# Program order on every engine for a seven-product encoder kernel, with its stages rewritten one run of twelve products apart

## The chip, the cores and the metric

The kernel runs on one core of one Trainium2 chip. The core has TensorE (PE in the profile; its weight loads are PEld), VectorE (DVE), ScalarE (ACT), GpSimd (POOL) and SyncE (SP, which here issues all DMAs). The engines work side by side and wait for each other through semaphores. The metric is the device time of one execution in microseconds, and lower is better.

## The reference

The reference is one layer of an encoder trunk on 2048 frames of 1024 features in float32. All branches read one normalised input through one projection, and their outputs go through one output projection:

```python
h = _rmsnorm(x, norm_w[layer])
proj = h @ w_in[layer]
...
y_a = _conv_mixer(a_h, a_b, a_c, a_z, conv_a_w[layer])
y_b = _gla_mixer(g_q, g_k, g_v, g_lr, g_z, gla_gate_w[layer], gla_gate_b[layer], gla_norm_w[layer])
y_c = _pool_mixer(p_u, p_z, pool_w[layer], pool_scale[layer])
y_d = _ssd_mixer(s_xbc, s_dt, s_z, ssd_conv_w[layer], ssd_conv_b[layer], ssd_dt_bias[layer],
                 ssd_a_log[layer], ssd_d[layer], ssd_norm_w[layer])
mix = jnp.concatenate([y_a, y_b, y_c, y_d], axis=-1)
x = x + mix @ w_out[layer]
...
return _rmsnorm(x, final_norm_w)
```

The conv branch is a causal convolution with gates. The gla and ssd branches carry a state from chunk to chunk of 64 frames (outer products within a chunk, a decayed sum over chunks, a product with the state). The pool branch takes running means over 2, 4, 8 and 16 frames. Each branch is gated by a SiLU of its own part of the projection.

## The kernel before

**Precision.** Every large product is made of three: both factors are split into a high and a low part (`split`: ACT casts the high part, DVE subtracts it to get the low part), and PE multiplies low by high, high by high and high by low. A product over 512 inputs is thus twelve matmuls of 128x512 (`mm12`, line 224), called a run here.

**Seven products.** Two projected blocks of 128 outputs, over two halves of 512 frames and two halves of the 1024 inputs, form a 2x2 block product. `pair7` makes it with seven runs instead of eight. `prep7` loads the four weight blocks of a pair, forms their sums on POOL (lines 200 to 210) and splits the seven left factors; the seven right factors (b11, t2, b21, t1, t3, t4, b22) stand in the dictionary `H`. `first7` makes the first run of the next pair ahead of time, into an accumulator a. Each pair begins by copying the negated a into a second accumulator b on ACT (line 240); b is then accumulated by three more runs, with a partial result read out between them (`cp2`, `cp3`, `ev21`), a by one more (`ev11`), and a third accumulator e by two (read by two subtractions, lines 252 and 262). A pair has 84 matmuls.

**Stages.** The frames go in two segments of 1024. In each segment a first phase multiplies by ordinary threes for the values, the gates and the time steps (`outer4`, `block_tok`), while `rows_gen` builds the right factors in `H`. Then follow the ten pairs of `PAIRS`: qk, B, xs, C (with a convolution and a SiLU each for the last three, `ssd_conv`), a_h, a_c, a_b, a_z (`a_pair`), p_u (`pu_pair`), p_z (`pz_pair`). From a_h on `chunk_loop` runs beside them: `update` makes a tile's state updates on PE, `advance` moves the states on by DVE and POOL, `outputs` multiplies by them on PE. `gate_outputs` norms and gates the results, and `to_mix` transposes them on PE and writes them to DRAM. After the second segment come eight more pairs, two rows of 128 frames each, for the output projection; `square` and `emit` make the last norm and write the rows. Their right factors come from `wout_gen`.

**Order.** The code is written as a series of runs with a call of `tick()` after each. A tick takes one step of each generator that is set (`chunks`, `prep_`, `side`) and then starts what `later(n, fn)` had put off by n ticks. So the program order mixes the work of several stages. It isn't the order of execution: a scheduler of the tile framework goes through the program with its own model of durations and puts each engine's instructions into an order, a ready instruction ahead of one that its model has still waiting. Only at few places is an order written by hand, with `issue_after` (`gate_decay`, `fin_B`). Whatever the order, an engine then runs its list one after the other.

The functions that the change touches, before it:

Of the kernel before, what the change touches and what calls it, by code (L numbers as in the profile page):

```python
# [9 lines left out]
F32 = mybir.dt.float32  # L10
# [7 lines left out]
P = 128  # L18
# [13 lines left out]
NW = 20  # L32
NG = 10
# [22 lines left out]
def tile_hybrid_trunk(ctx: ExitStack, tc: tile.TileContext, xtok, xT, wkv, wch, wpu, wz, wo, pw_, nw, par, gw, fnw, out):  # L56
    nc = tc.nc
    vec, act, pe, sp, pool = nc.vector, nc.scalar, nc.tensor, nc.sync, nc.gpsimd
# [134 lines left out]
    def prep7(load, w7):  # L193
# [4 lines left out]
        w7.append(split_w(a11))  # L198
# [4 lines left out]
        yield 1  # L203
        w7.append(split_w(s2))
        pool.tensor_add(a21, a21, a11)  # L205
        yield 1
        w7.append(split_w(a12))
        yield 1
        w7.append(split_w(a21))
        pool.tensor_add(a12, a12, s2)  # L210
        yield 1
        w7.append(split_w(s1))
        yield 1
        w7.append(split_w(a22))
        yield 1
        w7.append(split_w(a12))
        yield 1
# [10 lines left out]

    def first7(w7, H):

        a = acc()
        mm12(a, w7[0], H['b11'], True)
        ahead[0] = a
        tick()

    def pair7(w7, H, ev11, ev21, d12, d22, cp2, cp3, done, after=None):
# [12 lines left out]
        tick()  # L249
        e = acc()  # L250
        mm12(e, w7[4], H['t1'], True)
# [3 lines left out]
        mm12(b, w7[5], H['t4'], False)  # L255
# [3 lines left out]
        if after is not None:  # L259
            after()  # L260
        mm12(e, w7[6], H['b22'], False)
# [68 lines left out]
    def fold_pu(j):  # L330

        wt_ = [wt("wr", F32) for _ in range(2)]
        for h in range(2):
            sp.dma_start(wt_[h], wpu[j][:, h * 512:(h + 1) * 512])
# [3 lines left out]
        def fold(h):  # L338
            tp = tr()
            for i in range(4):  # L340
                pe.matmul(tp[:, i * P:(i + 1) * P], lhsT=wt_[h][:, i * P:(i + 1) * P], rhs=mix, start=True, stop=True)
# [4 lines left out]
        later(4, lambda: fold(1))  # L346
# [79 lines left out]
    def transposed(t, fn, lag=4):  # L426
# [8 lines left out]
    def chunk_loop(kv, kt, q, aG, aD, bt, xs, wt_, cc, after):  # L435
# [3 lines left out]
        def update(tt):  # L439
            wx = psm.tile([P, 4, CH], F32, tag="wx", name=nm("wx"), bufs=2)  # L440
# [3 lines left out]
            wx = wx.rearrange("p h c -> p (h c)")  # L444
# [39 lines left out]
        st = None  # L484
        for tt in range(TT):
            if tt:
                outputs(tt - 1, st)
            ups = update(tt)
            st = [advance(tt, i, ups[i]) for i in range(2)]
            for _ in range(TPT):  # L490
                yield 1
        outputs(TT - 1, st)

    def gate_outputs(s, f, kv, xs, rt):
# [4 lines left out]
        szs = []  # L499
        for i, tt in enumerate(ts4):  # L500
# [3 lines left out]
        ro = rsqrt(so.rearrange("p a b -> p (a b)"), 1.0 / CH, 16)  # L504
# [602 lines left out]
```

## Time and profile before

| | |
|---|---|
| Time, median of 3 runs | 871.24 us (869.7 to 872.1) |
| Time of the profiled execution | 871.0 us, of which 869.0 us is the span of the profile |
| Busy, of the span | PE 777.5 us, DVE 650.8 us, ACT 407.6 us, POOL 249.8 us |
| Mean granted TensorE clock | 0.955 |
| DMA | 94.08 MB, 108 GB/s |

The span reaches from the first to the last instruction. Busy time is the time in which an engine had an instruction under way; a matmul's end is modelled, and matmuls overlap. The first phase ends at 93.7 us, the first pair at 128.0, the other nine at 354.2; the second segment's first phase ends at 435.4, its ten pairs at 667.8. The output projection takes the rest.

### The profile page before, as it was taken

Reading aid. Unit: us, or ns where it says so; the run is one execution under the profiler, and the core shown is the slowest. Engines: PE = TensorE matmul, PEld = TensorE weight load, DVE = VectorE, ACT = ScalarE, POOL = GpSimd, SP = SyncE. Lnnn points to the kernel's source line nnn. Section 1 sums busy time; section 2 is a strip of 40 time slices with the busy share of each in tenths; the row PEclk is TensorE's granted clock in tenths of the full one; section 3 lists DMA queues with packets and bytes.
Section 4 is the critical chain, followed back from the end, with each engine's and each line's share of the span. In section 5 each row is a group of like instructions: output and inputs, shape, how many; then the busy total and the mean of one; then the engine's idle time right before and its main releaser. Section 6 shows DMA issues by size and latency. Waiting matters only on the chain. (4 is left out here: it accounts for less than half of the span.)

```text
span 869.0 us, 11534 instructions
## 1 busy us (share of the span) xinstructions
PE 777.5 (89%) x3944; PEld 628.3 (72%) x3944; DVE 650.8 (75%) x1252; ACT 407.6 (47%) x804; POOL 249.8 (29%) x206
## 2 busy tenths in 40 slices
PE   6999599999995998799999999989988479999985
PEld 5988378878774786687878877767867357777774
DVE  4779965776699689873835776797779988777775
ACT  6646526663562554353536664334554523333331
POOL 0003622335433120220322245543126522222200
PEclk9999799999998999979999999999989699999998
DMA  8611211121551543322041111112733624444411
GB/s 287 231 66 61 97 49 49 48 77 57 175 184 49 178 163 110 100 75 83 25 142 54 49 49 50 41 58 89 257 115 98 193 90 168 143 148 152 149 48 73
DMA packets 57578, 94.08 MB, mean 108 GB/s; under 512 B 5840, under 2 KB 20656, under 8 KB 57008
## 3 DMA queue, kind: packets, MB, share of 16 engines
q1 hardware_dynamic: 57520, 93.35, 32.4%
q8 instruction: 31, 0.51, 0.3%
q14 instruction: 27, 0.22, 0.1%
HBM read 71.31 MB, written 22.02 MB: 107 GB/s over the span
## 5 line engine op out<-in xcount | busy, mean ns | idle before, releaser
L224 PE MATMUL acc<-hl,wh 128*128 128x512 f32 x784 | 320.6, 409 | 52.8 <-DVE hl L151 22.7
L224 PE MATMUL acc<-hh,wl 128*128 128x512 f32 x784 | 312.4, 399 | 0.0
L224 PE MATMUL acc<-hh,wh 128*128 128x512 f32 x784 | 312.3, 398 | 0.0
L224 PEld LDWEIGHTS acc<-hl,wh 128*128 128x128 f32 x784 | 151.3, 193 | 95.7 <-DVE hl L151 16.9
L224 PEld LDWEIGHTS acc<-hh,wl 128*128 128x128 f32 x784 | 151.0, 193 | 33.0
L224 PEld LDWEIGHTS acc<-hh,wh 128*128 128x128 f32 x784 | 151.8, 194 | 29.4
L151 DVE TENSOR_TENSOR wl<-wr,wh 128x512 fp32r<-128x512 f32 (+1 forms) x172 | 119.9, 701 | 51.3 <-ACT wh L150 28.1
L150 ACT CAST wh<-wr 128x512 fp32r<-128x512 f32 (+1 forms) x172 | 101.7, 601 | 64.8 <-DVE wl L151 28.6
L200 POOL TENSOR_TENSOR ws<-wr,wr 128x512 f32<-128x512 f32 x28 | 42.5, 1520 | 272.9 <-PE acc L224 121.8
L151 DVE TENSOR_TENSOR wl<-ws,wh 128x512 fp32r<-128x512 f32 x56 | 42.8, 764 | 53.3 <-ACT wh L150 46.2
L150 ACT CAST wh<-ws 128x512 fp32r<-128x512 f32 x56 | 34.6, 618 | 92.6 <-POOL wr L205 55.3
L151 DVE TENSOR_TENSOR hl<-xq,hh 128x1024 fp32r<-128x1024 f32 (+1 forms) x52 | 72.6, 1426 | 2.2 <-ACT hh L150 2.1
L210 POOL TENSOR_TENSOR wr<-wr,ws 128x512 f32<-128x512 f32 x28 | 42.4, 1513 | 96.8 <-issue 77.2
L565 DVE SCALAR_TENSOR_TENSOR t<-xin,prm,t 128x512 f32<-128x512 f32 x72 | 58.3, 842 | 8.0 <-ACT t L563 8.0
L150 ACT CAST hh<-xq 128x1024 fp32r<-128x1024 f32 (+1 forms) x52 | 50.9, 1014 | 25.5 <-DVE xq L783 16.2
L302 PE MATMUL acc<-wl,hh 128*128 128x276 f32 (+1 forms) x160 | 55.5, 352 | 7.3 <-DVE wl L151 7.2
L966 ACT ACTIVATE xk<-r 128x512 f32<-128x512 f32 x32 | 20.2, 632 | 77.7 <-DVE r L1001 34.1
L302 PE MATMUL acc<-wh,hh 128*128 128x276 f32 (+1 forms) x160 | 50.0, 351 | 7.2 <-ACT wh L150 6.6
L302 PE MATMUL acc<-wh,hl 128*128 128x276 f32 (+1 forms) x160 | 54.4, 346 | 0.0
L783 POOL TENSOR_TENSOR xq<-xq,xq 128x1024 f32<-128x1024 f32 x10 | 28.9, 2896 | 62.7 <-DVE xq L783 48.5
L205 POOL TENSOR_TENSOR wr<-wr,wr 128x512 f32<-128x512 f32 x28 | 42.8, 1530 | 0.0
L302 PEld LDWEIGHTS acc<-wl,hh 128*128 128x128 f32 x160 | 32.5, 203 | 11.6 <-DVE wl L151 9.1
(219 smaller groups left out, 1104.8 us busy)
## 6 DMA issues: line engine op xcount, KB each, us to landing
wr<-in_wch SPq DMA_DIRECT2D x72, 256.0 KB, 3.4
xk<-in_xtok SPq DMA_DIRECT2D x64, 256.0 KB, 3.7
wr<-yd SPq DMA_DIRECT2D x32, 256.0 KB, 3.1
out<-r SPq DMA_DIRECT2D x32, 256.0 KB, 2.0
xq<-in_xT SPq DMA_DIRECT2D x14, 512.0 KB, 6.4
wr<-in_wz SPq DMA_DIRECT2D x16, 256.0 KB, 2.7
szd<-z SPq DMA_DIRECT2D x16, 256.0 KB, 2.4
sz<-szd SPq DMA_DIRECT2D x16, 256.0 KB, 3.1
```

The lines of the kernel that those rows point to most:

```text
L150: act.copy(hi, raw)
L151: vec.tensor_sub(lo, raw, hi.bitcast(F32))
L200: pool.tensor_add(s1, a21, a22)
L205: pool.tensor_add(a21, a21, a11)
L210: pool.tensor_add(a12, a12, s2)
L224: pe.matmul(o[:, cs], lhsT=a[:, ks], rhs=b[:, k, cs], start=start and k == 0 and i == 0, stop=k == KH - 1 and i == 2, skip_group_check=True)
L302: pe.matmul(o[tt][:, :n], lhsT=a[:, k % KH, sl], rhs=wts[k][b], start=k == 0 and i == 0, stop=k == KD - 1 and i == 2)
L565: vec.scalar_tensor_tensor(t, x[:, k:k + 512], pcol('scw', 4 * i + k), t, ALU.mult, ALU.add)
L783: eng.tensor_tensor(o[:, k:k + 2, :], x[:, k:k + 2, :], y[:, k:k + 2, :], op)
L966: act.activation(x[:, cs], r, AF.Square, accum_out=sq[:, i:i + 1])
```

## The change

**The order.** Each engine is wrapped in a class `Ordered`. While `strict[0]` is set, every instruction, DMA issues on SP and matmuls on PE among them, is tied behind the one that the program wrote before it on the same engine. It is set in each segment before its first pair, taken back after the first segment's last pair (so the second segment's first phase is ordered by the scheduler as before), and stays set from the second segment's pairs to the end. The `issue_after` in `fin_B` goes.

**The pair.** The seven runs of a pair, numbered here by the order in the new `pair7`, are: 1, s2 by t2 into b; 2, a12 by b21 into a; 3, s1 by t1 into e; 4, s3 by t3 into b; 5, the next pair's a11 by b11 (`first7`); 6, a22 by t4 into b; 7, s4 by b22 into e. A tick follows each, called tick 1 to 7. Before, run 4 stood ahead of run 3 and run 5 stood between 6 and 7. `prep7` issues its loads before the pair's first tick, does three of its four POOL sums in one step and makes one split per tick, and what is left is drained at the end of the pair, no longer before run 5.

**The rest.** `side` takes two steps per tick. Convolutions, SiLUs, transposes, the steps of `gate_outputs`, `emit` and `to_mix` get other distances in ticks. The chunk loop starts during C, takes two ticks per tile instead of three, and has `update` and `outputs` in different ticks; the tile `wx` has one buffer instead of two. `fold_pu` and `row_scale` for the second segment move from the pairs a_h and a_c into the first segment's first phase. The second segment's rows, or the output weights, are loaded and split from the end of a_z on. The weights of the second segment's first phase are fetched three ahead. The output pairs load their rows of x one pair ahead (`Rows`). The pool of 128x512 weight tiles goes from 20 to 18 buffers, the general one from 10 to 12. The arithmetic is the same.

```diff
-NW = 20
-NG = 10
+NW = 18
+NG = 12
...
+    strict = [False]
+    class Ordered:
...
+                if self.last is None:
+                    r = f(*args, **kw)
+                else:
+                    with tc.issue_after(self.last):
+                        r = f(*args, **kw)
+                self.last = r.ins
...
-        for g in (chunks, prep_, side):
+        for g in (chunks, prep_, side, side):
...
         a = ahead[0]
         b = acc()
         act.activation(b, a, AF.Copy, scale=-1.0)
-        mm12(b, w7[1], H['t2'], False)
+        mm12(b, w7['s2'], H['t2'], False)
         cp2(d12, b)
         tick()
-        mm12(a, w7[2], H['b21'], False)
+        mm12(a, w7['a12'], H['b21'], False)
         ev11(a)
         tick()
-        mm12(b, w7[3], H['t3'], False)
+        e = acc()
+        mm12(e, w7['s1'], H['t1'], True)
+        tick()
+        mm12(b, w7['s3'], H['t3'], False)
         cp3(d22, b)
-        tick()
-        e = acc()
-        mm12(e, w7[4], H['t1'], True)
         vec.tensor_sub(d22, d22, e)
         done(0)
         tick()
-        mm12(b, w7[5], H['t4'], False)
+        if after is not None:
+            after()
+            tick()
+        mm12(b, w7['a22'], H['t4'], False)
         ev21(b)
         done(1)
         tick()
-        if after is not None:
-            after()
-        mm12(e, w7[6], H['b22'], False)
+        mm12(e, w7['s4'], H['b22'], False)
         vec.tensor_sub(d12, e, d12)
         done(2)
         tick()
...
-    def transposed(t, fn, lag=4):
+    def transposed(t, fn, lag=2):
...
         st = None
+        wx = inputs(0)
+        yield 1
         for tt in range(TT):
             if tt:
                 outputs(tt - 1, st)
-            ups = update(tt)
+            yield 1
+            ups = update(tt, wx)
+            if tt + 1 < TT:
+                wx = inputs(tt + 1)
             st = [advance(tt, i, ups[i]) for i in range(2)]
-            for _ in range(TPT):
-                yield 1
+            yield 1
+        yield 1
         outputs(TT - 1, st)
...
-                later(1 + i, lambda tt=tt: to_mix(tt))
+                later(3 + i, lambda tt=tt: to_mix(tt))
...
+        later(3, scales_)
         for i, tt in enumerate(ts4):
-            later(1 + i, lambda i=i, tt=tt: gated(i, tt))
-        later(6, finish)
+            later(1 + i // 2, lambda i=i, tt=tt: squares(i, tt))
+            later(2 + i, lambda i=i, tt=tt: fetch(i, tt))
+            later(4 + i, lambda i=i, tt=tt: gated(i, tt))
+            later(5 + i, lambda i=i, tt=tt: sums(i, tt))
+        later(9, finish)
...
             for k in (2, 1, 0):
                 vec.scalar_tensor_tensor(t, x[:, k:k + 512], pcol('scw', 4 * i + k), t, ALU.mult, ALU.add)
-            fin(j, f, t)
+            later(1, lambda: fin(j, f, t))
...
             if j == 1:
-                conv(1, 1)
+                later(2, lambda: conv(1, 1))
             elif j == 2:
-                conv(0, 1)
+                later(2, lambda: conv(0, 1))
...
                 act.activation(t, u[:, 2:514], AF.Copy, scale=pcol('caw', 3 * j + 2))
-                for k in (1, 0):
-                    vec.scalar_tensor_tensor(t, u[:, k:k + 512], pcol('caw', 3 * j + k), t, ALU.mult, ALU.add)
+
+                def taps():
+                    for k in (1, 0):
+                        vec.scalar_tensor_tensor(t, u[:, k:k + 512], pcol('caw', 3 * j + k), t, ALU.mult, ALU.add)
+                later(1, taps)
...
                 elif j == 2:
-                    conv(0, 1)
+                    later(1, lambda: conv(0, 1))
...
-            with tc.issue_after(last_exp[0].ins):
-                act.activation(t, t, AF.Silu)
+            act.activation(t, t, AF.Silu)
...
+                    later(6, lambda: side.__setitem__(0, chain(next_wout(), pause(2), wout_gen(Hw))))
...
+        def done(self, j):
+            if j == 0:
+                square(self.r[1][1], self.x[1][1], self.sq[1], 0)
+            elif j == 1:
+                later(2, lambda: emit(self.tt + 1, self.rows[1], self.sq[1]))
+            else:
+                square(self.r[0][1], self.x[0][1], self.sq[0], 1)
+                if self.tt + 2 < NTT:
+                    later(3, lambda: emit(self.tt, self.rows[0], self.sq[0]))
+                else:
+                    emit(self.tt, self.rows[0], self.sq[0])
```

## Rows read from the trace of the kernel before

**Rows 1.** Busy time and clock by stretch; the columns stand in its first line.

```profile
core 0: us, PE busy (x) PEld busy (x) DVE busy (x) ACT busy (x) POOL busy (x), PEclk, DMA share, GB/s
...
93.70:128.00 34.30, 23.79 (x84) 18.27 (x85) 28.36 (x23) 14.51 (x22) 14.94 (x7) 0.80 0.27 89
128.00:354.20 226.20, 209.58 (x1171) 167.23 (x1171) 175.34 (x379) 123.61 (x252) 68.15 (x65) 0.97 0.33 107
354.20:435.40 81.20, 74.72 (x396) 65.15 (x395) 54.81 (x75) 34.49 (x64) 18.70 (x11) 0.94 0.24 71
435.40:667.80 232.40, 222.77 (x1202) 177.84 (x1201) 168.44 (x330) 113.51 (x224) 82.46 (x73) 0.98 0.28 94
667.80:711.20 43.40, 23.64 (x85) 17.96 (x84) 40.04 (x38) 19.62 (x28) 19.18 (x9) 0.84 0.38 117
711.20:840.90 129.70, 120.50 (x505) 96.10 (x504) 98.39 (x227) 43.91 (x98) 32.85 (x24) 0.97 0.40 140
```

**Rows 2.** PE's waits over the whole span: total, times, longest.

```profile
PE tr L529 <- DVE xs L521: 13.6, 3, 8.4
PE acc L224 <- DVE r L1010: 10.3, 6, 3.2
```

**Rows 3.** Timeline of PE from 271 us: start, length, instruction.

```profile
270.77 0.39 PE L224 MATMUL acc<-hh,wh 128*128 128x512 f32 x1
...
272.13 0.39 PE L224 MATMUL acc<-hh,wh 128*128 128x512 f32 x1
...
282.49 0.69 PE L529 MATMUL tr<-prm,xs 128*128 128x128 f32 x2 [8.35 <-DVE xs L521]
```

**Rows 4.** Groups on ACT by form: busy, mean ns, idle before.

```profile
L563 ACT ACTIVATE t<-xin,prm 128x512 f32<-128x512 f32 x24 | 18.9, 814 | 2.9 <-DVE xin L262 2.9
L240 ACT ACTIVATE acc<-acc 128x512 f32<-128x512 f32 x28 | 16.3, 582 | 9.8 <-PE acc L224 9.8
...
L611 ACT ACTIVATE ah<-u,prm 128x512 f32<-128x512 f32 x8 | 5.6, 717 | 3.2 <-DVE u L608 3.2
L899 ACT ACTIVATE t<-t 128x512 f32<-128x512 f32 x8 | 5.1, 633 | 2.9 <-DVE t L565 2.8
```

**Rows 5.** Timeline of DVE from 136 us.

```profile
147.49 4.11 DVE L565 SCALAR_TENSOR_TENSOR t<-xin,prm,t 128x512 f32<-128x512 f32 x6 [1.18 <-ACT t L563]
...
152.11 0.68 DVE L262 TENSOR_TENSOR xin<-acc,xin 128x512 f32<-128x512 f32 x1
```

**Rows 6.** Timeline of ACT from 710 us.

```profile
710.77 0.63 ACT L966 ACTIVATE xk<-r 128x512 f32<-128x512 f32 x1 [1.92 <-DVE r L1005]
711.31 0.18 ACT L966 ACTIVATION_READ_ACCUMULATOR xk<-r 128x1 f32 x1
711.40 0.58 ACT L240 ACTIVATE acc<-acc 128x512 f32<-128x512 f32 x1
711.92 0.60 ACT L150 CAST wh<-wr 128x512 fp32r<-128x512 f32 x1
```

**Rows 7.** Short stretches: a gap of PE and the time behind it.

```profile
583.00:586.50 3.50, 0.03 (x1) 0.00 (x0) 3.33 (x8) 1.01 (x4) 1.48 (x3) 0.99 0.00 0
586.50:589.90 3.40, 3.38 (x8) 2.70 (x9) 2.79 (x4) 2.58 (x5) 1.25 (x1) 0.51 0.02 5
```

**Rows 8.** Timeline of DVE from 655 us.

```profile
662.60 1.22 DVE L783 TENSOR_TENSOR xq<-xq,xq 128x1024 f32<-128x1024 f32 x1
...
668.29 2.31 DVE L783 TENSOR_TENSOR t<-xq,xq 128x1024 f32<-128x1024 f32 x1
...
684.84 14.54 DVE L151 TENSOR_TENSOR hl<-xq,hh 128x1024 fp32r<-128x1024 f32 x8
```

**Rows 9.** Timeline of DVE from 850 us, where the last row is written.

```profile
862.83 0.15 DVE L138 TENSOR_SCALAR na<-sq 128x1 int32<-128x1 int32 x1
...
864.56 1.41 DVE L976 SCALAR_TENSOR_TENSOR r<-r,ny,fw 128x512 f32<-128x512 f32 x2
```

**Rows 10.** Timeline of POOL from 655 us.

```profile
667.78 1.74 POOL L210 TENSOR_TENSOR wr<-wr,ws 128x512 f32<-128x512 f32 x1
```

More of the change, by code (lines that the diff above doesn't have):

```diff
@@ L345, in fold_pu @@
         later(2, lambda: fold(0))
-        later(4, lambda: fold(1))
+        later(3, lambda: fold(1))
     last_exp = [None]
@@ L498, in gate_outputs, with squares @@
         sy = psm.tile([P, 4], F32, tag="sy", name=nm("sy"))
-        szs = []
-        for i, tt in enumerate(ts4):
+        ro = []
+        szs = {}
+        def squares(i, tt):
             sq = gen("sq")[:, :256]
@@ L788, in chain, with pause @@
             yield from g
+    def pause(n):
+        for _ in range(n):
+            yield 1
     def half_gen(f):
@@ L879, in tile_hybrid_trunk @@
             spill_z(tt, o)
-        w7 = []
+        w7 = {}
         prep_[0] = prep7(load_pair(PAIRS[0]), w7)
+        if s + 1 < NSEG:
+            fold_pu(0)
+            later(3, lambda: fold_pu(1))
+            for f in range(2):
+                scales[2 * s + 2 + f] = psm.tile([P, 4], F32, tag="rt2", name=nm("rt2"))
+                later(2 + 3 * f, lambda f=f: row_scale(2 * s + 2 + f, scales[2 * s + 2 + f]))
         o = [acc() for _ in range(4)]
@@ L934, in tile_hybrid_trunk @@
                 prep_[0] = prep7(load_rows(0), w_next)
-            if name == 'a_h':
-                chunks[0] = chunk_loop(kv, kt, q, aG, aD, bt, xs, wt_, cc, after_chunks)
-                if s + 1 < NSEG:
-                    later(1, lambda: fold_pu(0))
-                    later(6, lambda: fold_pu(1))
-            if name == 'a_c' and s + 1 < NSEG:
-                for f in range(2):
-                    scales[2 * s + 2 + f] = psm.tile([P, 4], F32, tag="rt2", name=nm("rt2"))
-                    later(1 + 4 * f, lambda f=f: row_scale(2 * s + 2 + f, scales[2 * s + 2 + f]))
-            if name == 'p_u':
-                side[0] = next_rows(s + 1) if s + 1 < NSEG else next_wout()
-            if name == 'p_z':
-                drain(side)
-                side[0] = half_gen(0) if s + 1 < NSEG else wout_gen(Hw)
+            if w_next is not None and not (n + 1 == len(PAIRS) and s + 1 < NSEG):
+                next(prep_[0])
+            if name == 'C':
+                later(3, lambda: chunks.__setitem__(0, chunk_loop(kv, kt, q, aG, aD, bt, xs, wt_, cc, after_chunks)))
+            if name == 'a_z':
+                if s + 1 < NSEG:
+                    later(6, lambda: side.__setitem__(0, chain(next_rows(s + 1), pause(8), half_gen(0))))
+                else:
+                    later(6, lambda: side.__setitem__(0, chain(next_wout(), pause(2), wout_gen(Hw))))
             def after():
-                drain(prep_)
-                if w_next:
-                    first7(w_next, H if n + 1 < len(PAIRS) else Hw)
-            pair7(w7, H, *consumers(name), after=after)
+                first7(w_next, H if n + 1 < len(PAIRS) else Hw)
+            pair7(w7, H, *consumers(name), after=after if n + 1 < len(PAIRS) or s + 1 == NSEG else None)
+            drain(prep_)
             w7 = w_next
         drain(side)
+        strict[0] = s + 1 == NSEG
     NTT = SEQ // P
@@ L1022, in after @@
-        def after():
-            drain(prep_)
-            if w_next:
-                first7(w_next, H)
-        pair7(w7, H, ev11, ev21, r[0][1], r[1][1], cp2, cp3, done, after=after)
+            next(prep_[0])
+            later(3, lambda: nxt.append(Rows(tt + 2)))
+        rows.take()
+        pair7(w7, H, rows.ev11, rows.ev21, rows.r[0][1], rows.r[1][1], rows.cp2, rows.cp3, rows.done,
+              after=(lambda: first7(w_next, H)) if tt + 2 < NTT else None)
+        drain(prep_)
         w7 = w_next
+        rows = nxt[0] if nxt else None
@@ L1030, in _pack @@
+    while queue:
+        tick()
 def _pack(x, norm_w, w_in, conv_a_w, gla_gate_w, gla_gate_b, gla_norm_w, pool_w, pool_scale, ssd_conv_w, ssd_conv_b,
```

170 lines of the change are left out of this document (95 added, 75 removed).

## The prediction

> **What bounds the kernel now.** I read the busy time by stretch first, cut where the kernel's stages begin [rows 1]. PE is busy nearly throughout, so time is lost only where PE stands or runs at the lower clock. I count a stretch's loss as its length less PE's busy time, plus (1 - granted clock) times that busy time. It is 10.5 + 4.8 = 15.3 us in the first pair, 16.6 + 6.3 = 22.9 in the first segment's other nine, 6.5 + 4.5 = 11.0 in the second segment's first phase, 9.6 + 4.5 = 14.1 in its ten pairs, 19.8 + 3.8 = 23.6 in the first output pair, 9.2 + 3.6 = 12.8 in the next six: 99.7 us in all. The rest is matmuls that the change keeps.
>
> PE's waits say who is late [rows 2]: transposes that stood too early in PE's order for DVE, and the read of a partial result (cp2) on DVE. The timeline shows what one such place does [rows 3]: PE stood for 8.35 us at a transpose. From 270.77 to 272.13 us six matmuls start, one each 0.227 us, so a run takes 2.72 us.
>
> A gap also costs afterwards. PE stood for 3.5 us at clock 0.99, and the next 3.4 us ran at 0.51, the lower of the two levels (1.2 and 2.4 GHz) [rows 7]. That costs another 1.7 us.
>
> **What the change takes away.** The new stages put transposes two or more ticks behind what they read, and cp2 two runs ahead of the run that overwrites it. I count the losses of the three stretches of pairs as gone, 22.9 + 14.1 + 12.8 = 49.8 us (the rows leave 0 to 49.8). The weights of the second segment's first phase are split earlier: 7 of its 11.0 us. Two steps of `side` per tick bring the first pair's right factors forward, but DVE is busy for 28.4 of its 34.3 us [rows 1]: 7.3 of 15.3.
>
> The first output pair is a queue on DVE: eight low parts of right factors take 14.54 us in a row, 1.82 each [rows 8]. There are 14 of them and four sums for DVE. They move to nine ticks of p_u and p_z, two steps per tick, beside four window sums and the weight splits. Two steps at 1.22 to 1.82 are 2.4 to 3.6 us, a whole run for DVE before its other work. So most of the queue stays, now in p_u and p_z: I keep 14 of 23.6 us and take off 9.5. Gone in all: 49.8 + 7 + 7.3 + 9.5 = 73.6 us.
>
> The moved fold and `row_scale` (ACT squares, loads on SP) go at nothing: they are hidden by the first phase, where the same engines do them in place of later; if ACT is late there, the first pair gives back its 7.3. Two weight buffers fewer cost nothing either: two are freed with each run, and each tick takes two; if that is wrong, a split waits for one run, 2.72 us. Nothing in the rows prices DMAs in written order on SP. What stands behind a late spill is the next pair's four loads; their first use is a run away, and I take 0 (bound 2.72 per pair with a spill).
>
> **What the change adds.** The new wait is at the border of two pairs. Run 1 accumulates onto the negated copy that ACT writes at the start of the pair. Its input, run 5 of the pair before, is ready two runs earlier. Before, the copy could stand early in ACT's list; in one border it follows the square at once [rows 6]. Now it stands behind everything that the pair before wrote for ACT, up to tick 7, and some of that waits for run 6 or run 7. Behind it wait PE's run 1 and all later matmuls.
>
> *B and xs.* Behind run 6, ACT copies the result, applies the first tap, waits for DVE's three other taps, does the SiLU, then in tick 7 a cast and the next convolution's first tap, then the copy. With 0.58 for a copy, 0.81 for a first tap, 0.63 for a SiLU [rows 4], 4.11/6 = 0.685 per tap on DVE [rows 5] and 0.60 for a cast [rows 6]: 0.58 + 0.81 + 2.06 + 0.63 + 0.60 + 0.81 + 0.58 = 6.1 us. Run 7 covers 2.72 of it. PE stands 3.4 us.
>
> *C.* The same, and tick 7 has the first `outputs`, which waits for that SiLU, and whose result ACT copies before the negated copy: I take 4.4.
>
> *a_c.* The last product of DVE needs run 7, and in tick 7 DVE does two taps before it: subtraction 0.68, taps 1.37, product 0.68, ACT's tap 0.72 and the copy 0.58 make 4.0 [rows 4, 5]. Tick 6 also holds the last state update, two taps, a gating step and a product for DVE, which don't fit into one run. The nearest row above is the 8.35 us wait for DVE [rows 3]. I take 8, since both ticks are that full.
>
> *a_b and a_z.* At a_z: subtraction 0.68, SiLU 0.63, cast 0.60, copy 0.58, 2.5 after run 7; both have transposes of `to_mix` in tick 7 with their copies: 3.0 each (2.5 to 3.5). At qk, transposes, a copy and the negated copy: two copies behind PE, 1.2. At a_h nothing in tick 7 waits for run 7: 0, covered by run 7; without that cover, a copy, 0.6.
>
> One segment: 1.2 + 2 x 3.4 + 4.4 + 8 + 2 x 3.0 = 26.4, two 52.8. The border from p_z to the first output pair is like a_z without transposes, 2.6. In the output pairs the chain is subtraction 0.68, square and its accumulator 0.63 + 0.18, cast 0.60, copy 0.58 = 2.7, at seven borders 18.9.
>
> *Tail.* For the last two rows, row tt + 1 was written out during run 7. Now its `emit` stands in tick 7, behind the other row's. One takes from 862.83 to 865.97 us on DVE [rows 9]: 3.1, taken as 3.3 with its first steps' waits.
>
> *Smaller.* `update` and `outputs` in separate ticks break one more run per tile, at 0.2 for 16 tiles 3 us (an estimate between 0 and one lost start of 0.23 each). In p_u, 16 products for the next segment's rows fall into four ticks, 3 us of DVE each where a run lasts 2.72: 4. Against that, DVE and ACT catch up while PE stands at the borders, which I put at 4 to the good. Together: 52.8 + 2.6 + 18.9 + 3.3 + 3 + 4 - 4 = 80.6 us.
>
> *Clock.* Six of these gaps are as long as those after which the clock fell (four of 3.4, two of 8): 6 x 1.7 = 10. Sixteen are of 2 to 3 us; I let one in three pull the clock down, 9 (0 to 27). Together 19.
>
> Sum, on the profiled execution's own 871.0 us: 871.0 - 73.6 + 80.6 + 19 = 897. That execution stands 0.2 us from the median, 871.24, which needs no correction. I forecast 897 us.
>
> **Rivals.** *A, the borders are short.* The negated copy waits for a cast and itself only, 1.2 us at each of 23 borders, because ACT, held up nowhere else, works off its list in run 7's shade. For it: ACT is busy for only 407.6 of the 869 us, as the table above shows, and run 5 leaves two runs of slack. Against it: the chains above hold steps that can't begin before runs 6 or 7 end. Time: 871 - 73.6 + 27.6 + 10 (tail and smaller items) = 835. It decides once a border costs under (73.6 - 10)/23 = 2.8 us with its clock; I have 4.0. This is the case that ends faster.
>
> *B, DVE and POOL in each other's way.* The three sums of `prep7` now run in a row, at tick 1, where the convolutions' taps are. A DVE sum took 2.31 us from 668.29 on, while a POOL sum ran until 669.52, against 1.22 at 662.60 [rows 8, 10]. One such loss per pair adds 28 x 1.1 = 31: 928. The Trainium skill ("Trainium Architecture — The Big Picture", section "What this means for kernel authors") says that DVE and GpSimd share a port pair by an exclusive lock, so one stops rather than both slow down; by that rule each POOL sum in a row would stop DVE outright, and the loss would come out at this rival's end rather than at nothing. Against it: POOL does as many sums as before, and DVE has spare time in most ticks.
>
> *C, nothing changes.* The order already was near the program's, and old waits go over into new ones of the same size: 871. For it: PE loses only 11% in all.
>
> **Chances.** Forecast 0.55 (its own range 873 to 918, from half the border costs above their floors to the clock falling at every gap), A 0.27, B 0.13, C 0.05. A measurement of this kernel tells about 0.3% from no change, 2.6 us. Faster: A and the forecast's lower tail, 0.31; same 0.05; slower 0.64. The range goes from 848, which leaves half of A out, to 925, which leaves out half of B.
>
> **What would show it.** Right: ACT's group of negated copies (line 240 before) becomes PE's main releaser, one gap per border, 3 us and more at B, xs, C and a_c, about 2.7 in the output pairs; waits for cp2 and for the transposes of `to_mix` nearly vanish; p_u and p_z of the second segment get longer and the first output pair shorter. Wrong: PE passes from run 7 to run 1 without a gap, or gaps sit within pairs, at a transpose or an `outputs` that waits for DVE. The sum errs most on a_c, on the clock, and if the old waits don't vanish.

## The result, and the profile after

The changed kernel takes 1008.45 us (median of four runs, 1004.61 to 1012.62) against 871.67 (869.7 to 873.7) for the kernel before, run beside it: a ratio of 1.157, 95% interval 1.1516 to 1.1623. The profiled execution took 1012.62 us, of which 1010.8 us is the span. The forecast was 897, range 848 to 925: right in sign, and some 111 us short.

The changed kernel's busy time and clock, cut at the same places as [rows 1], with the first phase ahead of them:

```profile
core 0: us, PE busy (x) PEld busy (x) DVE busy (x) ACT busy (x) POOL busy (x), PEclk, DMA share, GB/s
0.00:110.40 110.40, 88.00 (x456) 74.46 (x456) 87.09 (x162) 72.83 (x154) 27.99 (x22) 0.89 0.55 183
110.40:132.60 22.20, 21.47 (x88) 17.34 (x89) 8.36 (x20) 7.98 (x15) 5.62 (x4) 0.93 0.31 106
132.60:401.10 268.50, 224.25 (x1145) 174.76 (x1144) 192.05 (x361) 110.01 (x217) 73.52 (x65) 0.93 0.23 73
401.10:476.60 75.50, 71.12 (x386) 62.19 (x385) 46.49 (x68) 33.27 (x60) 16.01 (x12) 0.95 0.22 69
476.60:769.00 292.40, 239.99 (x1201) 187.36 (x1200) 199.81 (x339) 115.76 (x226) 95.41 (x76) 0.92 0.22 73
769.00:802.20 33.20, 23.19 (x85) 18.26 (x86) 19.29 (x27) 14.20 (x23) 5.85 (x4) 0.79 0.40 135
802.20:975.10 172.90, 134.68 (x506) 105.82 (x505) 107.32 (x223) 43.04 (x96) 32.69 (x24) 0.88 0.33 109
975.10:1010.80 35.70, 21.46 (x85) 16.59 (x83) 18.98 (x56) 5.84 (x15) 0.00 (x0) 0.87 0.17 63
```

Set against [rows 1], three stretches carry nearly all: the first segment's nine pairs grew by 42.3 us, the second's ten by 60.0, the six output pairs by 43.2. The first phase grew by 16.7 us; the first pair, the second first phase and the first output pair became shorter by 12.1, 5.7 and 10.2. PE stands idle for 186.7 us (the span less PE's 824.15), before for 91.5. The busy time lost to the clock, (1 - clock) times PE's busy time summed over the stretches, is 73 us instead of 31. The two stretches of the kernel before that [rows 1] leaves out, its first phase and its end:

```profile
0.00:93.70 93.70, 83.27 (x425) 70.15 (x425) 69.51 (x135) 53.78 (x110) 13.57 (x20) 0.98 0.44 150
...
840.90:869.00 28.10, 19.22 (x85) 15.58 (x83) 15.97 (x48) 4.20 (x11) 0.00 (x0) 0.89 0.20 75
```

PE's waits in the changed kernel (total, times, longest). In the ordered stages the profile puts every instruction on line 76, the wrapper, so groups are told by their tiles:

```profile
PE acc L76 <- ACT acc L76: 76.7, 22, 8.7
PE acc L76 <- DVE r L76: 25.2, 8, 5.2
PE oy L76 <- POOL sb L76: 14.7, 12, 2.6
PE tr L71 <- DMA wu<-in_wpu: 12.4, 1, 12.4
PE acc L76 <- DVE pz L76: 10.2, 1, 10.2
PE acc L76 <- DVE wl L76: 8.1, 1, 8.1
```

The first row is the border of two pairs: run 1 waits for the negated copy. Of [rows 2], both waits are gone: no transpose waits for xs any more, and no run for `cp2`. The 25.2 us for r are another wait. There is one in each of the eight output pairs, at run 6, which adds onto run 4's result and so waits until DVE has read it (`cp3`); only run 5 stands between. The kernel before had this wait once:

```profile
PE acc L224 <- DVE r L1013: 2.3, 1, 2.3
```

Five rows of PE's timeline show the kinds (the bracket is the idle time ahead of the row and what ended it): the fold, the borders out of a_c, out of p_z and between two output pairs, and a wait for r.

```profile
105.43 2.90 PE L71 MATMUL tr<-mix,wu 128*128 128x128 f32 x12 [12.40 <-DMA wu<-in_wpu]
...
292.06 0.80 PE L76 MATMUL acc<-hl,wh 128*128 128x512 f32 x1 [8.67 <-ACT acc L76]
...
782.22 0.80 PE L76 MATMUL acc<-hl,wh 128*128 128x512 f32 x1 [8.57 <-ACT acc L76]
...
836.76 0.50 PE L76 MATMUL acc<-hl,wh 128*128 128x512 f32 x1 [2.53 <-ACT acc L76]
...
855.42 0.79 PE L76 MATMUL acc<-hl,wh 128*128 128x512 f32 x1 [3.14 <-DVE r L76]
```

ACT's timeline has what the second waited for, and a late cast ahead of the fifth:

```profile
290.80 0.72 ACT L76 ACTIVATE ah<-u,prm 128x512 f32<-128x512 f32 x1 [2.47 <-DVE u L76]
291.43 0.58 ACT L76 ACTIVATE acc<-acc 128x512 f32<-128x512 f32 x1
...
844.47 0.62 ACT L76 CAST wh<-wr 128x512 fp32r<-128x512 f32 x1 [7.76 <-DMA wr<-yd]
```

The border out of a_c is the chain of the forecast: ACT's last tap waits for DVE's product, the negated copy stands behind that tap, and PE stands for 8.67 us. The cast at 844.47 is another matter. SP's timeline shows why it is late, and why the fold in the first phase is:

```profile
95.48 0.33 SPq L71 DMA_DIRECT2D wd<-fw  x1
95.86 3.60 SPq L71 DMA_DIRECT2D xk<-in_xtok  x7
99.50 2.25 SPq L71 DMA_DIRECT2D wu<-in_wpu  x2
...
839.36 1.01 SPq L76 DMA_DIRECT2D out<-r  x2
840.46 1.83 SPq L76 DMA_DIRECT2D wr<-yd  x4
```

SP issues the next pair's four loads only when the two writes of finished rows, written ahead of them, could go; those wait for `emit`. The first cast of the loaded rows then waits for 7.76 us; DVE's list, whose next step is that cast's low part, comes 3 us late, and further down in it, behind the other row's `emit`, stands the reading of the partial result into r, for which PE waits at 855.42. In the first phase, which the scheduler still orders, seven loads of x stand ahead of the fold's weights wu, and ahead of these a write of the first half's result (wd), which follows its copy on ACT; in the 5.6 us before that write SP issued nothing.

### The profile page after: what moved, and what is told of

The parts are those of the page before. It is cut to its first block, busy times and chain, and to the rows that moved or that the text cites. A ratio compares the mean times of both kernels' runs of the same rounds, so it can differ in the third digit from the quotient of the medians.

```text
span 1010.8 us, 11513 instructions
## 1 busy us (share of the span) xinstructions
PE 824.1 (82%) x3944; PEld 656.8 (65%) x3944; DVE 679.4 (67%) x1252; ACT 402.9 (40%) x804; POOL 257.1 (25%) x206
## 5 line engine op out<-in xcount | busy, mean ns | idle before, releaser
L76 PE MATMUL acc<-hl,wh 128*128 128x512 f32 x782 | 335.8, 429 | 118.9 <-ACT acc L76 76.7
L76 PEld LDWEIGHTS acc<-hh,wh 128*128 128x128 f32 x784 | 159.8, 204 | 31.7
L76 DVE TENSOR_TENSOR wl<-wr,wh 128x512 fp32r<-128x512 f32 (+1 forms) x136 | 102.9, 757 | 82.0 <-ACT wh L76 74.5
L76 ACT CAST wh<-wr 128x512 fp32r<-128x512 f32 (+1 forms) x138 | 82.7, 604 | 62.4 <-DMA wr<-yd 53.1
L71 PE MATMUL acc<-wl,hh 128*128 128x512 f32 (+1 forms) x224 | 80.7, 364 | 8.2 <-DVE wl L76 7.4
L71 PE MATMUL acc<-wh,hl 128*128 128x512 f32 (+1 forms) x224 | 79.0, 358 | 0.0
L71 PE MATMUL acc<-wh,hh 128*128 128x512 f32 (+1 forms) x224 | 74.0, 363 | 4.8 <-ACT wh L71 4.8
L76 POOL TENSOR_TENSOR wr<-wr,ws 128x512 f32<-128x512 f32 x26 | 37.1, 1425 | 65.6 <-DVE wl L76 45.8
L71 PEld LDWEIGHTS acc<-wh,hh 128*128 128x128 f32 x224 | 41.9, 197 | 11.4 <-ACT wh L71 6.7
L71 PEld LDWEIGHTS acc<-wh,hl 128*128 128x128 f32 x224 | 44.6, 200 | 4.9
L71 DVE TENSOR_TENSOR hl<-xq,hh 128x1024 fp32r<-128x1024 f32 (+1 forms) x36 | 44.1, 1245 | 4.3 <-ACT hh L71 4.3
L71 ACT CAST hh<-xq 128x1024 fp32r<-128x1024 f32 (+1 forms) x36 | 35.1, 996 | 16.8 <-DVE xq L71 16.7
```

The source lines that it names most:

```text
L71: return f(*args, **kw)
L76: r = f(*args, **kw)
```

## The experiments

Times beside a run of the kernel before on the same chip (869.98 to 872.56 us); one run each, but for the last two versions. The four runs of the changed kernel itself lie 8 us apart, and those of the kernel before up to 5, so a difference of a few us between single runs tells nothing.

### The two halves of the change alone

The stages alone: the changed kernel, with the switch for the order never set.

```diff
-        strict[0] = True
+        strict[0] = False
...
-        strict[0] = s + 1 == NSEG
+        strict[0] = False
```

> The changed program, but the tie to program order is never set, so the scheduler orders it as it ordered the kernel before. Theory 'order' (the loss comes from each engine's list standing in program order): the gaps at the borders of pairs go, and the time falls back to 860 to 895 us, with the 12 us wait for the moved fold perhaps still there. Rival 'stages' (the rewritten stages themselves cost: the moved fold, the output weights' queue on DVE, fewer weight buffers): it stays above 960 us.

It took 891.43 us. So the new stages by themselves cost about 19 us, and the order on top of them 117.

The order alone: the kernel before with `Ordered` set over the same stages.

```diff
-    vec, act, pe, sp, pool = nc.vector, nc.scalar, nc.tensor, nc.sync, nc.gpsimd
+    vec, act, pe, sp, pool = [Ordered(e) for e in (nc.vector, nc.scalar, nc.tensor, nc.sync, nc.gpsimd)]
...
+        strict[0] = True
...
+        strict[0] = s + 1 == NSEG
```

> The kernel before with nothing changed but the tie to program order, set over the same stretches as in the change. Theory 'order': as slow as the changed kernel or slower, 1000 us and more, since this program was not written in stages. Rival 'stages': within 2% of 871 us.

It took 1118.23 us. The row of its longest wait (PE's waits):

```profile
PE acc L76 <- ACT acc L76: 218.8, 24, 24.2
```

With the old stages the border wait is nearly three times as long: under the written order the new stages are worth 110 us, and still not enough.

### One suspected wait at a time

The negated copy written behind tick 5, ahead of run 6:

```diff
...
+            ahead[1] = acc()
+            act.activation(ahead[1], ahead[0], AF.Copy, scale=-1.0)
         mm12(b, w7['a22'], H['t4'], False)
```

> The changed kernel with the negated copy written right behind tick 5, ahead of run 6, where run 5 has just been issued; all else stays. Theory 'copy behind late steps': PE's 76.7 us of waits for that copy go, and about 20 windows of half clock at 1.7 us with them: 900 to 930 us. Rival 'only the last wait in a row': the late steps of ACT and DVE hold PE at the next place (transposes, outputs, the reads of b), and less than 30 us is won: above 980 us.

It took 973.85 us, 34.6 less, between the two ranges: neither theory met it. The border wait of 76.7 us went, but PE's waits for r doubled, from 25.2 to 50.9 us, and all output pairs but the last stayed at 27 to 29 us. What makes r late there, SP's queue or DVE's list, this run doesn't tell apart.

SP left out of the order:

```diff
-    vec, act, pe, sp, pool = [Ordered(e) for e in (nc.vector, nc.scalar, nc.tensor, nc.sync, nc.gpsimd)]
+    vec, act, pe, pool = [Ordered(e) for e in (nc.vector, nc.scalar, nc.tensor, nc.gpsimd)]
+    sp = nc.sync
```

> The changed kernel with SP alone left to the scheduler, the other four engines still in program order. Theory 'loads behind writes on SP': in the eight output pairs the four weight loads no longer stand behind the rows' writes, the second gap per pair (25 us in all) goes with its half clock, 7 x 6 = 40 us less, and the first output pair gains too: 950 to 970 us. Rival 'DVE is simply late there': within 10 us of 1008.

It took 972.23 us, 36.2 less, 2 us outside the theory's range. The waits for r no longer stand among PE's longest, those for the negated copy stayed at 77.1 us, and an output pair took 23.7 us, with one gap of 2.5 where there had been two.

The fold and `row_scale` back in a_h and a_c:

```diff
-            fold_pu(0)
-            later(3, lambda: fold_pu(1))
...
+            if name == 'a_h' and s + 1 < NSEG:
+                later(1, lambda: fold_pu(0))
+                later(6, lambda: fold_pu(1))
```

> The changed kernel with only fold_pu and row_scale for the second segment put back into the pairs a_h and a_c. Theory: they cost the first phase 12.4 us of waiting for the loads of wu and about 4 us of the lower clock, and in a_h and a_c they cost little, since the chunk loop's work there is a queue on DVE and not on ACT: 990 to 996 us. Rival: under the written order they cost the same 16 us wherever they stand, since their loads, squares and transposes hold up what is written behind them: 1004 to 1012 us.

It took 1027.13 us, 18.7 more: both theories fell. The first phase and the first pair are together 3.8 us shorter (98.8 + 30.0), but a_c and a_b now take 42.9 and 43.9 us instead of 33.4 and 33.5, and one border wait reaches 19.7. Under the written order the fold is dearer there than in the first phase.

The inputs of the next tile written behind `advance`, which frees POOL earlier for `sb`:

```diff
-            if tt + 1 < TT:
-                wx = inputs(tt + 1)
             st = [advance(tt, i, ups[i]) for i in range(2)]
+            if tt + 1 < TT:
+                wx = inputs(tt + 1)
```

> The changed kernel with one step moved: the next tile's two POOL products stand behind the state's advance in POOL's list, no longer ahead of it. Theory 'POOL's list delays the state': of PE's 14.7 us of waits for the state sb about half goes, with two to four windows of half clock: 8 to 14 us less, 994 to 1000 us. Rival 'PE only waits for the copy instead': no change, within 3 us.

It took 995.78 us, 12.7 less, in the theory's range; of PE's waits for sb, though, only 4 of 14.7 us went.

### Several together

The early copy, SP free and the fold put back; then the inputs moved as well:

> The changed kernel with three repairs at once: the negated copy written behind tick 5, SP left to the scheduler, and the fold and row scales of the second segment put back beside the pairs a_h and a_c. Theory 'two lists held the output pairs, either one alone suffices': the gains add up to more than the single ones (34.6 and 36.2 us, and some 17 for the fold), since in the output pairs the early copy alone won little: 1008 - 35 - 36 - 17 - 25 = 895 us. Rival 'they overlap': 925 to 950 us.

> The three repairs and that step moved as well. Theory: 8 to 14 us below the run with three. What is left then is DVE's queue of output weights in the second segment's p_z, 20 us or more, and the first phase: 880 to 887 us.

They took 943.19 and 932.68 us. The first met the rival's range: more was left under the order than the three. The second came down by 10.5 us, as forecast, but its range of 880 to 887 was missed by 46. The largest waits left in it were for r (27.0 us) and for low parts and pz in p_z (19.4), all on DVE. So DVE was freed too:

> The kernel with the four repairs (negated copy written early, SP not ordered, fold put back, inputs after advance; 932.7 us) and VectorE not ordered either; TensorE, ScalarE and GpSimd stay in the written order. Theory: of the 143.8 us for which TensorE still stands there, VectorE's written order holds the output pairs (27 us of waits for r, where both rows' emit stands ahead of the partial results) and a part of the segments' pairs; the work of p_z and of the first output pair is a queue on VectorE in any order. So 895 to 910 us, with output pairs of 20.3 to 21.5 us instead of 24 to 25.7. Rival: VectorE is late by its load beside GpSimd and not by its order: 925 to 935 us, output pairs unchanged.

902.93 us, 29.8 less, as the theory had it; of the last seven output pairs five took 20.3 to 21.7 us, two still 23.6 and 24.9. Last, the same with the fold where the change has it:

> The kernel with the negated copy written early, inputs after advance, SyncE and VectorE not ordered, and the fold where the change has it (with the fold put back this was 902.9 us). Theory: under ScalarE's written order the fold costs more in a_h and a_c, where its copies and squares stand ahead of the chain that TensorE waits for, than the 12.4 us of waiting for its loads in the first phase: 886 to 898 us. Rival: with SyncE and VectorE free it costs the same in both places: 900 to 906 us.

893.85 us, 9 less, again the theory's case. It is 2.4 us above the stages alone, which single runs don't resolve; and since the stages alone lack the early copy and the moved inputs, this isn't the price of ACT's, PE's and POOL's order by itself.

### One engine's list at a time

The stages of the change, with one engine alone held to the written order.

```diff
+    pe, = [Ordered(e) for e in (nc.tensor,)]
+    vec, act, pool, sp = nc.vector, nc.scalar, nc.gpsimd, nc.sync
```

> The changed kernel with TensorE alone held to the written order in the same stretches; VectorE, ScalarE, GpSimd and SyncE are free. Theory: the cost is the lists of the engines that feed TensorE (negated copy, SP's queue, emit), not the order of its matmuls, which in these stages is written far enough behind: 893 to 910 us, near the 891.4 us of the stages alone. Rival: half of the cost of the order lies in TensorE's own list, since it stops at each transpose or outputs that is late instead of going on with the next run: 940 to 960 us.

> The new stages with ScalarE alone held to the written order. Theory: ScalarE's list carries the border waits by itself, since the chain that the prediction counted (copy, tap, SiLU, cast, negated copy) needs nothing of the other lists: 891 plus 60 to 85 us, so 950 to 975, with TensorE waiting for the negated copy at nearly every border. Rival: the chains are long only because VectorE's and SyncE's lists are fixed too: 891 to 915 us.

> The new stages with VectorE alone held to the written order. Theory: freeing it took 30 us where TensorE, ScalarE and GpSimd were held, above all where emit and state updates stand ahead of what TensorE waits for; alone it costs about as much: 912 to 930 us. Rival: alone its list can be made up for by the other engines: 891 to 900 us.

> The new stages with SyncE alone held to the written order, so that its DMAs are issued in the order of the program. Theory: the output pairs stay long, since the four loads of y stand behind the writes of out whatever the other engines do: 915 to 930 us, with output pairs of 24 to 28 us instead of 20.3. Rival: the writes of out are late only because VectorE's emit is late in its own written order, so with VectorE free SyncE's list costs nothing: 888 to 896 us.

TensorE alone took 891.49 us: its order costs nothing that shows. ACT alone took 919.83 (+28.4), between the two ranges and nearer the rival's; DVE alone 927.45 (+36.0) and SP alone 926.45 (+35.0), both as the theory had it. By stretch, in us of each profiled execution:

| | stages alone | ACT held | DVE held | SP held | all held |
|---|---|---|---|---|---|
| first phase and first pair | 135.4 | 131.0 | 133.8 | 135.0 | 132.6 |
| nine pairs | 231.4 | +8.4 | +8.7 | +7.3 | +37.1 |
| second first phase | 75.4 | 73.9 | 72.3 | 74.1 | 75.5 |
| ten pairs | 260.4 | +8.9 | +0.8 | +4.1 | +32.0 |
| first output pair | 33.5 | 35.0 | 37.8 | 39.9 | 33.2 |
| six output pairs | 122.3 | +13.0 | +23.9 | +18.5 | +50.6 |
| last | 31.3 | 33.7 | 34.3 | 31.7 | 35.7 |

PE's waits with ACT alone held, the first row; then with SP alone held, the first two (r of line 1075 is read by `cp2`, of line 1078 by `cp3`):

```profile
PE acc L241 <- ACT acc L76: 32.0, 16, 9.1
```

```profile
PE acc L241 <- DVE r L1075: 17.9, 1, 17.9
PE acc L241 <- DVE r L1078: 17.3, 7, 3.7
```

With DVE and SP free, the border waits are 32.0 us at 16 places instead of 76.7 at 22. SP's list makes PE wait for r with every other list free. The wait of 17.9 us is in the first output pair; in the stages alone it is 11.5. SP's timeline has what stands ahead of that pair's loads, four writes of p_z's results, issued over 23.55 us as they become ready:

```profile
709.37 23.55 SPq L76 DMA_DIRECT2D yd<-pz  x4
732.98 0.99 SPq L76 DMA_DIRECT2D fw<-in_fnw  x2
```

### The stages themselves

The stages alone with the fold put back, then also the inputs moved and transposes four ticks behind again:

```diff
...
-    def transposed(t, fn, lag=2):
+    def transposed(t, fn, lag=4):
...
```

> The new stages without the tie to program order, and the fold and row scales put back. Theory 'the moved fold costs its wait': 15.9 us of PE's waits for the fold's weights go with their half clock, 891 falls to 870 to 876 us, level with the kernel before. Rival 'the wait moves on to the first pair's right factors on DVE': 885 us and more.

> The new stages in the scheduler's order with the fold put back (891.1 us), and two more distances taken back: transposes four ticks behind what they read instead of two, inputs of the next tile behind advance. Theory: this takes away TensorE's 9.2 us of waits for t at its transposes, 4.9 for kd and about half of the 8.5 for sb, with some of the lower clock behind them: 868 to 878 us. Rival: the scheduler puts other instructions in their place and TensorE waits elsewhere, as it did when the fold was put back: 885 to 893 us.

They took 891.14 and 885.70 us, both in the rival's range. The first lost its 14.3 us wait for wu and got one of 9.2 us for the last z ahead of the first pair; in the second the 9.2 us of waits for t no longer stand among the longest. Three stretches of the second, the nine pairs, the ten and the six output pairs:

```profile
132.20:368.20 236.00, 217.90 (x1170) 170.24 (x1169) 186.30 (x383) 123.35 (x253) 73.98 (x66) 0.97 0.33 107
443.70:697.30 253.60, 231.31 (x1200) 180.47 (x1201) 183.85 (x334) 117.24 (x227) 87.45 (x74) 0.97 0.25 84
730.90:852.60 121.70, 115.99 (x505) 94.13 (x504) 102.64 (x223) 44.08 (x96) 35.41 (x24) 1.00 0.44 148
```

Counted as in the forecast, they lose 18.1 + 6.5 = 24.6 us, 22.3 + 6.9 = 29.2 and 5.7, against 22.9, 14.1 and 12.8 before. Of these only the output pairs gained, and beside them the second first phase (75.5 us against 81.2). The first output pair is 9.8 us shorter than before, but the ten pairs ahead of it are 21.2 us longer.

### A version faster than both

So these two parts alone, on the kernel before and in the scheduler's order, run six times:

```diff
+            if i < KD:
+                raws_.append(fetch_kv(i))
+            if i >= 3:
+                wk.append(split_w(raws_[i - 3], KVN))
...
+    xn = [load_x(0), load_x(1)]
...
-        xa, xb = load_x(tt), load_x(tt + 1)
+        xa, xb = xn
+        if tt + 2 < NTT:
+            later(4, lambda t=tt: xn.__setitem__(slice(0, 2), [load_x(t + 2), load_x(t + 3)]))
...
+                later(2, lambda t=tt + 1, r=r2, q=sb_: emit(t, r[:, 1, :], q))
...
+                    later(3, lambda t=tt, r=r2, q=sa: emit(t, r[:, 0, :], q))
```

> The kernel before in the scheduler's order with two parts of the change alone: the weights of the second segment's first phase fetched three ahead, and in the output pairs the rows of x loaded one pair ahead and emit put off by two or three ticks. Theory: these two parts gained 5.7 us in the second segment's first phase and about 5 us in the output pairs where the stages ran alone, and bring as much here: 859 to 864 us against 871. Rival: the gains there came from the shape of the new pairs and of side, not from these parts: 868 to 873 us.

865.93 us against 871.35: a ratio of 0.9931, interval 0.9906 to 0.9955. That is 0.7% faster than the kernel before, small but clear of the noise, and by about half of what was expected: it lies between the theory's range and the rival's. Four stretches, to be set against [rows 1]: nine pairs, second first phase, ten pairs, six output pairs:

```profile
128.00:358.90 230.90, 212.53 (x1172) 169.12 (x1172) 175.84 (x380) 123.91 (x255) 68.72 (x65) 0.96 0.34 108
358.90:435.70 76.80, 73.01 (x396) 63.08 (x395) 50.93 (x74) 34.60 (x63) 18.92 (x11) 0.96 0.23 74
435.70:665.10 229.40, 221.56 (x1201) 176.69 (x1200) 168.22 (x330) 113.06 (x223) 82.54 (x73) 0.99 0.28 92
...
708.50:835.60 127.10, 117.77 (x505) 93.64 (x504) 96.47 (x222) 44.01 (x98) 32.58 (x24) 1.00 0.41 143
```

The second first phase gains 4.4 us, the ten pairs 3.0, the output pairs 2.6, and the nine pairs, where the weights are now fetched, give back 4.7; that the fetching is what costs there was not tried.

On top of it, the low parts of t4 and b22 of the output projection on POOL:

```diff
...
+                eng.tensor_tensor(lo, raw[:, k:k + 2, :], hi.bitcast(F32), ALU.subtract)
...
-            yield from split_gen(H, n, r)
+            yield from split_gen(H, n, r, pool if n in ('b22', 't4') else None)
```

> The version with the two parts alone (865.9 us), and the low parts of the last two right factors of the output projection, t4 and b22, subtracted by GpSimd instead of VectorE. Four of 14 low parts of 1.82 us leave VectorE's list. Theory: the wait at the first output pair is VectorE's own work, so up to 7.3 us come off: 858 to 862 us, the first output pair 36 to 39 us instead of 43.3. Rival: GpSimd takes 3.3 us for a tile of 128x1024 and VectorE stands beside it, so nothing is gained: 865 to 870 us.

865.86 us (ratio to the kernel before 0.993, 0.9906 to 0.9954): the rival's case, the first output pair even 46.3 us long instead of 43.4. Its timeline, DVE and then POOL:

```profile
675.57 1.21 DVE L151 TENSOR_TENSOR hl<-xq,hh 128x1024 fp32r<-128x1024 f32 x1
...
679.51 13.24 DVE L151 TENSOR_TENSOR hl<-xq,hh 128x1024 fp32r<-128x1024 f32 x4
```

```profile
681.76 13.22 POOL L786 TENSOR_TENSOR hl<-xq,hh 128x1024 fp32r<-128x1024 f32 x4
```

While POOL made its four, DVE's four took 3.31 us each instead of 1.21.

## Why the prediction was right or wrong

Its terms by stretch, its clock apart, against what was measured, the clock's share included. All 26.4 us of a segment's borders are counted to its pairs:

| | forecast | measured |
|---|---|---|
| first phase | 0 | +16.7 |
| first pair | -7.3 | -12.1 |
| nine pairs | -22.9 + 26.4 + 1.5 = +5.0 | +42.3 |
| second first phase | -7 | -5.7 |
| ten pairs and first output pair | -14.1 - 9.5 + 26.4 + 2.6 + 1.5 + 4 = +10.9 | +49.8 |
| six output pairs | -12.8 + 16.2 = +3.4 | +43.2 |
| last | 2.7 + 3.3 = +6.0 | +7.6 |
| anywhere: catch-up, clock | -4 + 19 | |
| sum | +26.0 | +141.8 |

**Right: the border wait, in mechanism and size.** The negated copy became PE's main releaser. The forecast's borders sum to 52.8 + 2.6 + 18.9 = 74.3 us, PE waited for 76.7; a_c stood at 8.67 us for 8, an output pair at 2.53 for 2.7. That the sums meet so closely is partly luck: the border out of C took 2.18 us for 4.4, that out of p_z 8.57 for 2.6, since the output's right factors kept DVE busy there. Right, too, were the second first phase, the tail, and that waits for `cp2` vanish. The first pair is right in sign only: the first phase ahead of it grew, and the two together are 4.6 us longer. And gaps inside pairs, which the prediction named as a sign of being wrong, came as well, if at other places: 25.2 us for r, 14.7 at `outputs` for POOL's sb, 18.3 in p_z.

**But that wait was not one list's.** Held alone, ACT cost 28.4 us, and the copy written early gave back 34.6. The chains that the forecast summed run over DVE's steps, and DVE's place in them was fixed as well. When one list is freed, the next one's wait takes over: 25.2 us became 50.9.

**Failed: "I count the losses of the three stretches of pairs as gone", 49.8 us.** In the scheduler's order, and with the fold, the inputs and the transposes' distance put back, the new stages still lose 24.6 + 29.2 + 5.7 = 59.5 us there, and with nothing put back 23.6 + 36.6 + 6.1 = 66.3. Some of it is the queue that moved into p_z (below); the rest are other waits in the old ones' place, for sb, for kd, for b. This is the costliest of the failed steps if one goes by the two halves: the forecast took 73.6 us off for the stages and put 80.6 + 19 on, nearly all for the order, and measured were 19 more for the stages and 117 for the order. So some 90 of the missing 111 us lie with the stages and some 20 with the order, an estimate, for the halves don't simply add: under the written order the new stages are worth 110 us. The rival C, old waits going over into new ones, describes the stages alone better than the forecast did.

**Failed: SP in written order at nothing.** The bound was 2.72 us per pair with a spill, on the ground that the loads' first use is a run away. What stood ahead of them in the output pairs was not a spill but the rows' last writes, which wait for `emit`; spills stood only ahead of the first output pair's loads. SP's list costs 35.0 us alone, and 36.2 came off when it was freed. Of the 35.0 us, 18.5 lie in the six output pairs, which the bound left out altogether, and 6.4 in the first, more than twice the bound.

**Failed: DVE's written order had no term.** Its steps entered only as links of ACT's chains, and what DVE does while PE stands was booked as 4 us to the good. `cp3`, one run ahead of the run that waits for it, was not priced. Alone its list costs 36.0 us, 23.9 of them in the six output pairs.

These three lists alone cost 28.4 + 36.0 + 35.0 = 99.4 of the 117 us. The other 17.6 are shown by no single run: GpSimd's list was not run alone. For a joint effect of the lists speak the two stretches of segment pairs, where single lists sum to 24.4 and 13.8 us, and all together cost 37.1 and 32.0. That the version with ACT, PE and POOL held and the copy early ends within 2.4 us of the stages alone fits this, but doesn't show it. How much is POOL's stays open.

**Failed: the clock.** One in three of the gaps of 2 to 3 us was to pull the clock down, and six gaps were to be longer. In the changed kernel there are 19 of 2 to 3 us, of which 14 have a stretch at the lower level at them or right behind, and 19 longer ones, all with one. The term was 19 us, with part of the old losses to the clock counted as gone; the busy time lost to it rose by 42 us. The term has a slip too, which changes little: the borders listed are 22, not 23, and the two out of C, at 4.4, belong to the long gaps; counted so, it is 13.6 + 6.8 = 20.4 us.

**Half right: the output's right factors.** I kept 14 us of the queue and took 9.5 off. The first output pair now loses 10.0 + 4.9 = 14.9, but p_z, with the rest of the queue, has 39.3 us for its 19.0 us of matmuls. In the stages alone p_z and the first output pair together lose 9.2 + 15.9 = 25.1 us. Before, p_z lost nothing, and the pair 23.6: nothing came off. The two stretches of the stages alone, then p_z before:

```profile
674.60:702.50 27.90, 21.30 (x85) 16.78 (x84) 27.90 (x28) 10.79 (x16) 12.09 (x6) 0.88 0.12 38
702.50:736.10 33.60, 22.11 (x86) 17.70 (x86) 29.43 (x34) 16.03 (x26) 16.72 (x7) 0.80 0.50 162
```

```profile
648.10:667.80 19.70, 19.70 (x92) 16.30 (x91) 19.70 (x23) 10.14 (x22) 8.88 (x5) 1.00 0.40 121
```

**Wrong reason: the moved fold at nothing.** What came late were the loads in SP's queue, which the prediction had hidden by the first phase, and that phase grew by 16.7 us. But putting it back cost 18.7 us under the full order and 9 with SP and DVE free, and in the scheduler's order made no difference. So the move isn't a part of the loss.

**The rival B** is seen in places. DVE's timeline in p_z and in an output pair, and POOL's beside it, in the changed kernel:

```profile
730.56 0.71 DVE L76 TENSOR_TENSOR A<-X 128x526 f32<-128x526 f32 x1 [0.26 <-ACT X L76]
...
743.48 2.81 DVE L76 TENSOR_TENSOR A<-X 128x526 f32<-128x526 f32 x1
...
837.94 0.16 DVE L76 SCALAR_TENSOR_TENSOR ny<-na,ny 128x1 f32<-128x1 f32 x1
...
849.61 1.22 DVE L76 SCALAR_TENSOR_TENSOR ny<-na,ny 128x1 f32<-128x1 f32 x1
```

```profile
743.38 5.13 POOL L76 TENSOR_TENSOR xq<-xq,xq 128x1024 f32<-128x1024 f32 x2
...
849.52 1.29 POOL L76 TENSOR_TENSOR wr<-wr,wr 128x512 f32<-128x512 f32 x1
```

The same sum took 2.81 us beside POOL and 0.71 without it, a step of `emit` 1.22 and 0.16. `emit` grows by some 2.7 us in this way, ahead of the r for which PE waits at 855.42. What that costs in all was not measured by itself.

## What to carry to other kernels

Before writing an order by hand, price each engine's list alone, the DMA queue's first: ask of every issue what stands ahead of it and what that waits for. Don't book a gap's length as its worth: where several lists are late at nearly the same time, taking one wait away only shows the next. And try the parts of a rewrite one by one on the old kernel: two of them were worth 0.7% in an order that was left alone.

## What the runs showed of the hardware

DVE and POOL took turns rather than work side by side: with four low parts on each, both lists took 13.2 us, 3.31 for a pair, where one alone is 1.21 on DVE (in [rows 8], where POOL had sums for a part of the time, it was 1.82). So POOL's own part of a turn would be 2.1 us (an estimate, the difference), and giving it four of the 14 low parts gained nothing. The Trainium skill ("SBUF — State Buffer", section "SBUF: two separate sides") says that the two engines' shared port pair is locked for a whole instruction, the other engine blocking; these rows agree with that, and with it even a step on 128x1 paid for a POOL sum's length.

PE's waits cost again by the clock: in the whole kernel 95 us more of standing came with 42 us more lost to the lower level, 0.44 us for each. The widest border, as [rows 7] show a gap of before, in two short stretches of the changed kernel:

```profile
283.40:292.10 8.70, 0.04 (x1) 0.04 (x1) 6.82 (x15) 2.85 (x6) 0.00 (x0) 0.75 0.29 90
292.10:295.50 3.40, 3.40 (x8) 2.72 (x9) 0.00 (x0) 0.00 (x0) 0.00 (x0) 0.50 0.00 0
```

The clock fell while PE stood, and the run behind the gap went at 0.50, the lower level of 1.2 GHz.
